# Layer 0's FFN sums through four PSUM banks, modulation products on ACT, layer 1's values and probabilities in float32

## The chip, the core and the metric

The kernel runs on one core of one Trainium2 chip. The core has TensorE (PE, with its own queue for weight loads, PEld), VectorE (DVE), ScalarE (ACT), GpSimd (POOL) and SyncE (SP), which here issues nearly all transfers from HBM, in the order of its queue. The metric is the time of one execution on the device in microseconds (us); less is better.

## The reference, cut to what matters

Two layers work on 512 latent tokens and 256 context tokens of width 1024. Both end in a SwiGLU FFN with 2816 hidden channels; layer 1's mixer is a differential attention with 8 heads of 2 x 64. In layer 1 the context gives only keys and values.

```
mx = silu(c) @ mod_w[l] + mod_b[l]          # shift, scale, gate, twice; the context has its own
h  = rms(x) * (1 + scale) + shift
q, k, v = split(h @ w_in)                   # layer 1, per head 2 x 64, 2 x 64 and 128
q, k = rope(rms(q) * qn), rope(rms(k) * kn) # rope on the latent tokens only
a  = softmax(q0 k0 / 8) - lam * softmax(q1 k1 / 8)
x  = x + gate1 * (rms(a @ v) * subln * (1 - lam_init)) @ w_out
x  = x + gate2 * ((silu(h @ w_gate) * (h @ w_up)) @ w_out)
```

## The kernel before, in words

The 768 tokens are six tiles of 128 (t = 4, 5 are the context). Nearly every product is made in three parts: weight and operand are each split into a high half (a cast to fp32r by ACT, L303 for weights, L397 for operands) and a low half (a subtraction by DVE or POOL, L304 and L398), and PE multiplies high by high, high by low and low by high. Attention weights times values in layer 0 are plain float32.

The order of the instructions on each engine is not written by hand: a scheduler with a cost model sets it from the order of the program, from priorities and from the number of buffers behind each tile name. SP issues transfers in the order it was given; one that waits for a buffer holds up all behind it.

The stages by time are layer 0's mixer (to about 450 us), layer 0's FFN (to 1048), layer 1's input projections and attention (1048 to 1400), its output projection and the norm before the FFN (to 1492) and layer 1's FFN (to the end).

The FFN (`ffn`, L710) goes over 22 blocks of 128 hidden channels in 11 passes of two. For each block PE makes the gate product `pg` and the up product `pu` (L738, 24 matmuls with 512 columns, and in layer 0 24 more with the context's 256) in two PSUM tiles of two banks each (`p_sc`, the names take turns). ACT makes Silu of `pg` into `sg`, DVE multiplies `sg` by `pu` (L753), and `split` makes the two halves `hdh` and `hdl`. Then each token tile and half of the columns gets its sum `dps` (L771 to L773, six matmuls of 512 columns, twelve in the last sums, which join two passes), in the banks `acc0` and `acc1` in turn. `residual` (L388) multiplies it by the gate into a tile `rtmp` in SBUF (DVE, L391) and adds that to x (L392: DVE, or POOL for the joined sums of layer 0). Two more PSUM banks, `tr0` and `tr1`, are there for transposes and small matmuls.

During layer 0's FFN the modulations of layer 1 are computed from 96 loads of 512 KB in all (`modw`, L191; some belong to the earlier path). `mod_chunks_by_pool` (L182) works for each chunk of 256 columns through two halves of the rows, for one or two streams (latent and context, the second in `modp`, one buffer; `modw` has two): POOL multiplies [128 x 4 x 256] by the conditioning vector (L197) and adds the four parts (L198 to L203) into `ma`. A matmul with ones (`modrow`, L208) sums over the partitions, ACT copies the row (L213), and a matmul turns it into columns (`modcol`, L216). `MODS1` gives the number of chunks for each pass: 2, 2, 2, 2, 2, 3, 3, 4, 4; the first eight chunks have two streams. There are 64 units of chunk, half and stream.

Layer 1 has a head's input projection (`in_proj1`, L571) for each token tile: the sum `inps` is copied to `qkv` by ACT, the values are split (`vv`: cast by ACT L594, subtraction by POOL L595), and `qk_norm_rope` squares (ACT, L358), reduces (DVE, L360), takes 1/sqrt on POOL (`rs_q`, L148 and L149), multiplies by it on DVE (L363), then multiplies by the rotation tables (`qz`, L372, and `qy`, L374, for queries and for keys each) and adds (L375). Queries and keys are then split and transposed on PE (`qpt`, L613, and `kpt`, L619). `attend1` (L625) makes two score tiles per head and latent tile, the exponentials `e` on ACT, their difference on DVE (L646), six transposes into `ppt`, a split of these into `PTh` and `PTl` (ACT and DVE), and the sum `av` (L653, L654) in six pairs of matmuls: `PTh` by both halves of the values side by side (256 columns) and `PTl` by the high half (128 columns). Two operations (ACT L656, DVE L658) join the two halves into `o`. Weights of the next head are loaded and split meanwhile (`wir`, L303 and L304).

## Time and profile before

| what | value |
|---|---|
| median of three runs | 1863.59 us (1863.56 to 1865.19) |
| profiled execution | 1865.25 us, its span 1863.5 us |
| PE busy | 1760.2 us (94%) |
| DVE, POOL, ACT busy | 1162.2, 789.8 and 716.5 us (62, 42 and 38%) |
| HBM read | 159.73 MB, 88 GB/s over the span |

The span is the time from the first to the last instruction in the trace; the rest of the profiled execution lies around it. Busy time counts an engine's own work, without its waits. The "chain that ended last" follows the work back from the last instruction. In the groups of instructions, the number behind the bar is the idle time of the engine just ahead of those instructions, with the instruction that ended it. "Granted clock" is the share of its full speed at which PE ran in a stretch.

### The profile page before, as it was taken

How to read it: one execution, taken by the hardware profiler on the slowest of the kernel's cores; microseconds unless marked ns; L12 is line 12 of the kernel's file. 1: busy time of each engine (PE TensorE's matmuls, PEld its weight loads, DVE VectorE, ACT ScalarE, POOL GpSimd, SP SyncE). 2: the span in 40 equal slices, each digit the busy share in tenths (PEclk: the TensorE clock that was granted, in tenths of full speed). 3: DMA queues.
4: the chain of work that ended last, by engine and by line, in shares of the span. 5: the costliest groups of instructions: out<-in, count | busy, mean ns of one | idle time of the engine just before them, and what ended most of it. 6: DMA issues, size and time to landing. Idle time of an engine off the chain costs nothing.

```text
span 1863.5 us, 25986 instructions
## 1 busy us (share of the span) xinstructions
PE 1760.2 (94%) x9910; PEld 1459.6 (78%) x9910; DVE 1162.2 (62%) x1927; ACT 716.5 (38%) x1470; POOL 789.8 (42%) x852
## 2 busy tenths in 40 slices
PE   6999999998999999899999889999998899999998
PEld 4877776666778888788888788999886688888887
DVE  4665455445268876667771767888876556566563
ACT  6556555434211112112211555676665332222220
POOL 2864545521099986735561655655543200000000
PEclk9999999999999999999999889999999899999999
DMA  9112222302533234424330211111103133223231
GB/s 314 42 41 77 83 93 91 100 23 81 180 114 101 93 100 146 138 91 136 103 124 14 96 38 57 35 38 48 49 19 107 46 113 108 85 91 113 69 113 46
DMA packets 152477, 165.64 MB, mean 89 GB/s; under 512 B 16480, under 2 KB 139936, under 8 KB 152352
## 3 DMA queue, kind: packets, MB, share of 16 engines
q1 hardware_dynamic: 152000, 163.77, 27.6%
q8 instruction: 78, 1.28, 0.3%
q14 instruction: 47, 0.39, 0.1%
q10 hardware_dynamic: 352, 0.21, 0.0%
HBM read 159.73 MB, written 4.22 MB: 88 GB/s over the span
## 4 chain that ended last, share of the span: by engine, by line
PE 74%; DVE 9%; ACT 5%; POOL 4%; DMA 3%; issue 3%; SPq 0%; POOLq 0%; ACTq 0%; DVEq 0%
PE pg L738 14%; PE pu L738 14%; PE dps L771 5%; PE dps L773 5%; PE dps L772 5%; PE inps L384 4%; PE inps L385 3%; PE inps L386 3%; PE av L548 3%; PE ppt L538 2%; PE sc L504 2%; PE ops L705 2%; PE ops L707 2%; PE ops L706 2%; PE av L653 1%
## 5 line engine op out<-in xcount | busy, mean ns | idle before, releaser
L738 PE MATMUL pg<-hT,wgh 128*128 128x512 f32 (+1 forms) x720 | 246.6, 391 | 3.1 <-ACT hT L288 3.1
L738 PE MATMUL pu<-hT,wuh 128*128 128x512 f32 (+1 forms) x720 | 243.2, 388 | 0.0
L391 DVE TENSOR_TENSOR rtmp<-dps,g 128x512 f32<-128x512 f32 x200 | 135.8, 687 | 163.7 <-PE dps L773 162.0
L392 DVE TENSOR_TENSOR x<-x,rtmp 128x512 f32<-128x512 f32 x188 | 198.8, 1065 | 3.8
L771 PE MATMUL dps<-wdh,hdh 128*128 128x512 f32 x440 | 177.1, 403 | 2.2 <-DVE rtmp L391 2.2
L772 PE MATMUL dps<-wdl,hdh 128*128 128x512 f32 x440 | 174.8, 397 | 0.0
L773 PE MATMUL dps<-wdh,hdl 128*128 128x512 f32 x440 | 171.9, 398 | 1.6 <-DVE hdl L398 1.6
L738 PEld LDWEIGHTS pg<-hT,wgh 128*128 128x128 f32 x720 | 135.4, 190 | 34.4 <-ACT hT L288 3.3
L738 PEld LDWEIGHTS pu<-hT,wuh 128*128 128x128 f32 x720 | 134.2, 188 | 29.6
L738 PE MATMUL pg<-hT,wgl 128*128 128x512 f32 (+1 forms) x360 | 141.4, 393 | 0.0
L738 PE MATMUL pu<-hT,wul 128*128 128x512 f32 (+1 forms) x360 | 139.7, 388 | 0.0
L384 PE MATMUL inps<-wih,hT 128*128 128x384 f32 x384 | 132.9, 346 | 0.4 <-ACT qkv L446 0.2
L397 ACT CAST hdh<-sg 128x768 fp32r<-128x768 f32 (+1 forms) x44 | 32.0, 728 | 256.5 <-DVE sg L753 256.5
L386 PE MATMUL inps<-wih,hT 128*128 128x384 f32 x384 | 130.3, 339 | 0.0
L385 PE MATMUL inps<-wil,hT 128*128 128x384 f32 x384 | 130.2, 339 | 0.0
L197 POOL TENSOR_TENSOR modw<-modw,cols 128x1024 f32<-128x1024 f32 x48 | 100.8, 2103 | 54.0 <-DMA modw<-in_mod_w_dram 53.7
L738 PE MATMUL pg<-hTc,wgh 128*128 128x256 f32 x352 | 99.5, 287 | 3.1 <-ACT hTc L288 2.4
L528 POOL TENSOR_SCALAR Pt<-Pt,rc 128x256 f32<-128x256 f32 (+3 forms) x96 | 69.2, 733 | 77.0 <-DVE rc L525 64.9
L771 PEld LDWEIGHTS dps<-wdh,hdh 128*128 128x128 f32 x440 | 83.2, 189 | 23.0 <-DVE rtmp L391 3.4
L773 PEld LDWEIGHTS dps<-wdh,hdl 128*128 128x128 f32 x440 | 83.0, 189 | 22.2 <-DVE hdl L398 2.3
L738 PE MATMUL pu<-hTc,wuh 128*128 128x256 f32 x352 | 98.1, 283 | 0.0
L772 PEld LDWEIGHTS dps<-wdl,hdh 128*128 128x128 f32 x440 | 83.3, 189 | 17.5
(230 smaller groups left out, 4486.3 us busy)
## 6 DMA issues: line engine op xcount, KB each, us to landing
modw<-in_mod_w_dram SPq DMA_DIRECT2D x96, 512.0 KB, 4.3
wgr<-in_ffn_w_in_dram SPq DMA_DIRECT2D x44, 512.0 KB, 3.4
wur<-in_ffn_w_in_dram SPq DMA_DIRECT2D x44, 512.0 KB, 3.5
wdr<-in_ffn_w_out_dram SPq DMA_DIRECT2D x44, 512.0 KB, 3.6
wir<-in_od_w_in_dram SPq DMA_DIRECT2D x96, 128.0 KB, 2.2
x<-in_x_dram SPq DMA_DIRECT2D x8, 512.0 KB, 3.5
wir<-in_ev_w_in_dram SPq DMA_DIRECT2D x16, 256.0 KB, 2.7
wor<-in_ev_w_out_dram SPq DMA_DIRECT2D x8, 512.0 KB, 4.3
```

Source lines behind the costliest of these rows:

```text
L197: nc.gpsimd.tensor_tensor(pr, w, bc(sk, 2, width), ALU.mult)
L384: nc.tensor.matmul(ps, hs[0][:, k, :], a, start=k == 0, stop=False)
L385: nc.tensor.matmul(ps, hs[0][:, k, :], b, start=False, stop=False)
L386: nc.tensor.matmul(ps, hs[1][:, k, :], a, start=False, stop=k == KT - 1)
L391: nc.vector.tensor_mul(tmp, ps, g[:, n * 512:(n + 1) * 512])
L392: eng.tensor_add(xt[:, n * 512:(n + 1) * 512], xt[:, n * 512:(n + 1) * 512], tmp)
L528: nc.gpsimd.tensor_scalar(p[:, :n], p[:, :n], rc[:, hh:hh + 1], 1.0, ALU.mult, ALU.mult)
L548: nc.tensor.matmul(av[64 * j:64 * j + 64, :], vv[:, vt[kc], :], PT[:, 2 * j:2 * j + 2].rearrange("p h q -> p (h q)"), start=kc == 0, stop= ...
L738: nc.tensor.matmul(ps[:, s0:s1], a, cols_T(b, s0, s1)[:, k, :], start=k == 0 and q == 0, stop=k == KT - 1 and q == 2)
L771: nc.tensor.matmul(ps, hh, a, start=j == 0, stop=False)
L772: nc.tensor.matmul(ps, hh, b, start=False, stop=False)
L773: nc.tensor.matmul(ps, hl, a, start=False, stop=j == nj - 1)
```

## The change

Four things are changed.

1. In both FFNs `sg` times `pu` is written back into `pu` in PSUM, and `split` reads it there; the residual multiplies `dps` in place and DVE adds it to x from PSUM (no `rtmp`, and no POOL adds for the joined sums). The sums of two blocks go through four banks, `acc0`, `tr0`, `acc1`, `tr1`; the joined sums keep two.
2. Of the modulations' work, the multiplications go from POOL (64 of 128 x 1024) to ACT (256 of 128 x 256, with a column of the conditioning vector as scale). The additions stay on POOL.
3. Layer 1's rotation tables hold all four 64-wide heads (two of queries, two of keys) with their norm weights (`head_tables`, in place of `rope_tables`), so that `rotate_all` has one multiplication for `qz` and one for `qy`, on the values that are not normalised yet. The multiplication by `rs_q` follows on POOL.
4. Layer 1's values are kept in float32 (a copy by POOL), and so are the transposed attention probabilities (the first four tiles copied by ACT, the last two by DVE). `av` is made of six float32 matmuls of 128 columns, and ACT alone scales it into `o`.

The scheduler orders the changed program anew. In layer 0's mixer PE's order stays as it was.

```diff
--- before.py
+++ after.py
@@ -75,7 +75,7 @@
     p_sc = es.enter_context(tc.tile_pool(name="p_sc", bufs=2, space=PSUM))
     dram = es.enter_context(tc.tile_pool(name="dram", bufs=1, space=bass.MemoryType.DRAM))
     p_1 = es.enter_context(tc.tile_pool(name="p_1", bufs=1, space=PSUM))
-    turn = {"acc": 0, "tr": 0}
+    turn = {"acc": 0, "tr": 0, "sum": 0}
 
     def phase_pool(name, side="left"):
         return tc.tile_pool(name=name, bufs=1, side=side, reuse_waits="tile")
@@ -193,8 +193,9 @@
                 for i, acc in reversed(list(enumerate(accs))):
 
                     pr = pool.tile([P, 4, width], F32, name="modp", tag="mp", bufs=1) if i else w
-                    sk = cols[:, 8 * i + 4 * pc:8 * i + 4 * pc + 4]
-                    nc.gpsimd.tensor_tensor(pr, w, bc(sk, 2, width), ALU.mult)
+                    for k in range(4):
+                        kk = 8 * i + 4 * pc + k
+                        nc.scalar.activation(pr[:, k], w[:, k], AF.Copy, scale=cols[:, kk:kk + 1])
                     nc.gpsimd.tensor_add(pr[:, 0:2], pr[:, 0:2], pr[:, 2:4])
                     if pc == 0:
                         nc.gpsimd.tensor_add(acc, pr[:, 0], pr[:, 1])
@@ -326,6 +327,45 @@
                                     rp[:, :, 1, :].rearrange("p t (a b) -> p t a b", b=2),
                                     bc(sw, 1, NTX), ALU.mult)
         return w, tb
+
+    def head_tables(pool, wq, wk, nq, nk):
+
+        rp = raw_tile([P, NTX, 2, HD], "rp")
+        nc.sync.dma_start(rp, rope)
+        n = nq + nk
+        w = pool.tile([P, 2, 2, HD], F32, name="rw", tag="rw")
+        nc.sync.dma_start(w[:, 0, 0, :], dram_rows(wq))
+        nc.sync.dma_start(w[:, 0, 1, :], dram_rows(wk))
+        nc.vector.tensor_scalar(w[:, 0, 0, :], w[:, 0, 0, :], HD ** -0.5, None, ALU.mult)
+        for j in range(2):
+            nc.vector.tensor_copy(w[:, 1, j, :].rearrange("p (a b) -> p a b", b=2), swap_pairs(w[:, 0, j, :]))
+        tb = pool.tile([P, NTX, 2, n, HD], F32, name="rt", tag="rt")
+        wc = pool.tile([P, n, HD], F32, name="rc", tag="rc")
+        for j, h0, m in ((0, 0, nq), (1, nq, nk)):
+            nc.vector.tensor_copy(wc[:, h0:h0 + m], bc(w[:, 0, j, :], 1, m))
+            for i in range(2):
+                wj = bc(bc(w[:, i, j, :], 1, m), 1, NTX)
+                nc.vector.tensor_tensor(tb[:, :, i, h0:h0 + m], bc(rp[:, :, i, :], 2, m), wj, ALU.mult)
+        return wc, tb
+
+    def rotate_all(raw, h0, n, t, wc, tb, pool):
+
+        sq = pool.tile([P, n * HD], F32, name="sq", tag="qz", bufs=2)
+        nc.scalar.activation(sq, raw, AF.Square)
+        ss = small.tile([P, n], F32, name="qss", tag="qss")
+        nc.vector.tensor_reduce(ss, sq.rearrange("p (h d) -> p h d", d=HD), AX.X, ALU.add)
+        r = rsqrt(ss, n, 1.0 / HD, "q")
+        y = pool.tile([P, n, HD], F32, name="qy", tag="qy", bufs=2)
+        rh = raw.rearrange("p (h d) -> p h d", d=HD)
+        if t >= NTX:
+            nc.vector.tensor_tensor(y, rh, wc[:, h0:h0 + n], ALU.mult)
+            return y, r
+        z = pool.tile([P, n, HD], F32, name="qz", tag="qz", bufs=2)
+        nc.vector.tensor_tensor(z.rearrange("p h (a b) -> p (h a) b", b=2),
+                                swap_pairs(raw), tb[:, t, 1].rearrange("p h (a b) -> p (h a) b", b=2), ALU.mult)
+        nc.vector.tensor_tensor(y, rh, tb[:, t, 0], ALU.mult)
+        nc.vector.tensor_add(y, y, z)
+        return y, r
 
     def rotate(raw, nq, nk, t, w, tb, pool):
 
@@ -351,30 +391,6 @@
         nc.vector.tensor_add(y, y, z)
         return y, r
 
-    def qk_norm_rope(ps, nq, nk, t, w, tb, pool):
-
-        n = nq + nk
-        sq = pool.tile([P, n * HD], F32, name="sq", tag="qz", bufs=2)
-        nc.scalar.activation(sq, ps[:, :n * HD], AF.Square)
-        ss = small.tile([P, n], F32, name="qss", tag="qss")
-        nc.vector.tensor_reduce(ss, sq.rearrange("p (h d) -> p h d", d=HD), AX.X, ALU.add)
-        r = rsqrt(ss, n, 1.0 / HD, "q")
-        y = pool.tile([P, n, HD], F32, name="qy", tag="qy", bufs=2)
-        nc.vector.tensor_tensor(y, ps[:, :n * HD].rearrange("p (h d) -> p h d", d=HD), bc(r, 2, HD), ALU.mult)
-        parts = [p for p in ((0, 0, nq), (1, nq, nk)) if p[2]]
-        if t >= NTX:
-            for j, h0, m in parts:
-                nc.vector.tensor_tensor(y[:, h0:h0 + m], y[:, h0:h0 + m], bc(w[:, j, :], 1, m), ALU.mult)
-            return y
-        z = pool.tile([P, n, HD], F32, name="qz", tag="qz", bufs=2)
-        for j, h0, m in parts:
-            sn = tb[:, j, t, 1, :].rearrange("p (a b) -> p a b", b=2)
-            nc.vector.tensor_tensor(z[:, h0:h0 + m].rearrange("p h (a b) -> p h a b", b=2),
-                                    swap_pairs(y[:, h0:h0 + m]), bc(sn, 1, m), ALU.mult)
-            nc.vector.tensor_tensor(y[:, h0:h0 + m], y[:, h0:h0 + m], bc(tb[:, j, t, 0, :], 1, m), ALU.mult)
-        nc.vector.tensor_add(y, y, z)
-        return y
-
     def project(ps, t, ws, c0, c1):
 
         hs = [tile_T(j, t) for j in range(2)]
@@ -397,22 +413,6 @@
         nc.scalar.copy(hi, src)
         nc.vector.tensor_sub(lo, src, f32(hi))
         return hi, lo
-
-    def transposed_probs(Pt, heads, tiles, pool):
-
-        res = []
-        per = 4 // heads
-        for g0 in range(0, len(tiles), per):
-            grp = tiles[g0:g0 + per]
-            m = len(grp)
-            pt = tr_tile("ppt", [P, per, heads, P])
-            for a, kc in enumerate(grp):
-                for hh in range(heads):
-                    nc.tensor.transpose(pt[:, a, hh, :], Pt[hh][:, kc * P:(kc + 1) * P], ident)
-            hi, lo = split(pool, pt[:, :m], [P, m, heads, P], "PT", 2)
-            for a in range(m):
-                res.append((hi[:, a], lo[:, a]))
-        return res
 
 
     def weights0(b, wp, sub, new_tile=raw_tile):
@@ -569,7 +569,7 @@
         return nlam
 
     def in_proj1(h, tabs, wp, st, wh, qp):
-        w, tb = tabs
+        wc, tb = tabs
         ws = []
         for u in range(4):
             def views(raw, u=u):
@@ -579,21 +579,22 @@
                         "(j p) n -> p j n", p=P)
             ws.append(unit(wh, views, [P, 2, 384], WBUF, "wi", nc.gpsimd if h or u % 2 else nc.vector))
         kT = st.tile([P, 2, TOK], F32R, name="kT", tag="kT")
-        vv = st.tile([P, NT, 2, P], F32R, name="vv", tag="vv")
+        vv = st.tile([P, NT, P], F32, name="vv", tag="vv")
         qs = {}
         late = None
         yield qs, kT, vv
         for t in CTX_FIRST:
-            nq = 2 if t < NTX else 0
-            n = 384 if nq else 256
+            h0 = 0 if t < NTX else 2
+            m = 4 - h0
+            n = 64 * m + P
             ps = acc_tile("inps", n, one=0) if h else p_sc.tile([P, 1024], F32, name="inps", tag="sc")[:, :n]
             project(ps, t, ws, 384 - n, 384)
             raw = wp.tile([P, 384], F32, name="qkv", tag="qkv", bufs=2)
             nc.scalar.copy(raw[:, :n], ps)
-            v = raw[:, n - P:n]
-            nc.scalar.copy(vv[:, t, 0, :], v)
-            nc.gpsimd.tensor_sub(vv[:, t, 1, :], v, f32(vv[:, t, 0, :]))
-            y = qk_norm_rope(raw, nq, 2, t, w, tb, wp)
+            nc.gpsimd.tensor_copy(vv[:, t, :], raw[:, n - P:n])
+            y, r = rotate_all(raw[:, :n - P], h0, m, t, wc, tb, wp)
+            nc.gpsimd.tensor_tensor(y, y, bc(r, 2, HD), ALU.mult)
+            nq = m - 2
             if nq:
                 qd = wp.tile([P, 2, 2, 2, HD], F32R, name="qd", tag="qd", bufs=2)
                 yb = bc(y[:, 0:2], 2, 2)
@@ -645,18 +646,24 @@
         nc.vector.scalar_tensor_tensor(rt, sm[:, 0:1], nlam, rc[:, 1:2], ALU.mult, ALU.mult)
         nc.vector.scalar_tensor_tensor(E[0], E[1], rt, E[0], ALU.mult, ALU.add)
         yield
-        PT = transposed_probs(E[:1], 1, list(range(NT)), mp)
-        av = acc_tile("av", 256, one=1)
+        av = acc_tile("av", P, one=1)
         vt = [4, 5, 0, 1, 2, 3]
-        for a, (hi, lo) in enumerate(PT):
-            v = vv[:, vt[a]].rearrange("p a d -> p (a d)")
-            nc.tensor.matmul(av, hi[:, 0], v, start=a == 0, stop=False)
-            nc.tensor.matmul(av[:, 0:P], lo[:, 0], v[:, 0:P], start=False, stop=a == len(PT) - 1)
+        for g0, m in ((0, 4), (4, 2)):
+            pt = tr_tile("ppt", [P, 4, P])
+            for a in range(m):
+                nc.tensor.transpose(pt[:, a, :], E[0][:, (g0 + a) * P:(g0 + a + 1) * P], ident)
+            PT = mp.tile([P, 4, P], F32, name="PT", tag="PT", bufs=3)
+            if g0:
+                nc.vector.tensor_copy(PT[:, :m], pt[:, :m])
+            else:
+                nc.scalar.copy(PT, pt)
+            for a in range(m):
+                kc = g0 + a
+                nc.tensor.matmul(av, PT[:, a, :], vv[:, vt[kc], :], start=kc == 0, stop=kc == NT - 1)
+        oc = o_t[t][:, h * P:(h + 1) * P]
+        nc.scalar.activation(oc, av, AF.Copy, scale=rc[:, 0:1])
+        ss = small.tile([P, 1], F32, name="oss", tag="oss")
         o1 = mp.tile([P, P], F32, name="o1", tag="o1", bufs=2)
-        nc.scalar.activation(o1, av[:, P:2 * P], AF.Copy, scale=rc[:, 0:1])
-        oc = o_t[t][:, h * P:(h + 1) * P]
-        nc.vector.scalar_tensor_tensor(oc, av[:, 0:P], rc[:, 0:1], o1, ALU.mult, ALU.add)
-        ss = small.tile([P, 1], F32, name="oss", tag="oss")
         nc.scalar.activation(o1, oc, AF.Square, accum_out=ss)
         r = rsqrt(ss, 1, 1.0 / P, "o")
         nc.vector.scalar_tensor_tensor(oc, oc, r, subln, ALU.mult, ALU.mult)
@@ -750,8 +757,9 @@
                 pg, pu = pg[:, :n_tok], pu[:, :n_tok]
                 sg = fp.tile([P, n_tok], F32, name="sg", tag="sg", bufs=1)
                 nc.scalar.activation(sg, pg, AF.Silu)
-                nc.vector.tensor_mul(sg, sg, pu)
-                hid.append(split(fp, sg, [P, n_tok], "hd", 4))
+
+                nc.vector.tensor_mul(pu, sg, pu)
+                hid.append(split(fp, pu, [P, n_tok], "hd", 4))
             for i, mod in enumerate(mods[0] if p == 0 and mods else ()):
                 mod_chunk(*mod, lambda shape, name: fp.tile(shape, F32, name=name, tag="mw", bufs=2), fp, f"tr{i % 2}", room=("ma", 4))
             if p and mods and mods[p]:
@@ -764,14 +772,18 @@
             nj = len(hid)
             for t in CTX_FIRST[:ntok] if ntok > NTX else range(ntok):
                 for n in range(2):
-                    ps = acc_tile("dps")
+                    if nj > 2:
+                        ps = acc_tile("dps")
+                    else:
+                        turn["sum"] = (turn["sum"] + 1) % 4
+                        ps = p_1.tile([P, 512], F32, name="dps", tag=("acc0", "tr0", "acc1", "tr1")[turn["sum"]])
                     for j in range(nj):
                         hh, hl = (z[:, t * P:(t + 1) * P] for z in hid[j])
                         a, b = (z[:, n * 512:(n + 1) * 512] for z in wo[j])
                         nc.tensor.matmul(ps, hh, a, start=j == 0, stop=False)
                         nc.tensor.matmul(ps, hh, b, start=False, stop=False)
                         nc.tensor.matmul(ps, hl, a, start=False, stop=j == nj - 1)
-                    residual(xs[t], ps, g[0 if t < NTX else 1], n, fp, nc.gpsimd if nj > 2 and l == 0 else nc.vector)
+                    residual(xs[t], ps, g[0 if t < NTX else 1], n)
                     if p == NF // 2 - 1:
                         done(t, n)
             wo, hid = [], []
@@ -932,7 +944,7 @@
     wp = Pool("mw1", "right")
     whi = Pool("whi", "right")
     wh = (whi.pool, wlo.pool)
-    tabs = rope_tables(wp.pool, od_qn[0], od_kn[0])
+    tabs = head_tables(wp.pool, od_qn[0], od_kn[0], 2, 2)
     fp.close()
     at = Pool("mix1")
     subln = at.pool.tile([P, P], F32, name="subln")
```

## The prediction

> **What bounds the kernel now.** I read the busy table and the chain of waits first, then one row per stage of the busy-time view (window in us, its length, then busy time of PE, PEld, DVE, ACT and POOL with counts, then the granted TensorE clock).
>
> ```profile
> PE 1760.2 (94%) x9910; PEld 1459.6 (78%) x9910; DVE 1162.2 (62%) x1927; ACT 716.5 (38%) x1470; POOL 789.8 (42%) x852
> ...
> PE 74%; DVE 9%; ACT 5%; POOL 4%; DMA 3%; issue 3%; SPq 0%; POOLq 0%; ACTq 0%; DVEq 0%
> ```
> ```profile
> 0.00:516.00 516.00, 474.36 (x3039) 357.03 (x3040) 256.58 (x583) 257.91 (x575) 221.21 (x302) 0.99 0.32 102
> 516.00:1048.00 532.00, 520.91 (x2746) 439.53 (x2745) 361.10 (x383) 103.00 (x120) 351.40 (x244) 0.99 0.33 104
> 1048.00:1160.00 112.00, 96.35 (x578) 90.65 (x577) 76.97 (x162) 60.67 (x148) 59.42 (x78) 0.86 0.22 65
> 1160.00:1384.00 224.00, 215.45 (x1493) 205.83 (x1492) 187.87 (x409) 151.43 (x418) 126.32 (x195) 1.00 0.12 36
> 1384.00:1492.00 108.00, 86.74 (x461) 70.88 (x461) 70.59 (x126) 53.26 (x105) 31.49 (x37) 0.91 0.22 75
> 1492.00:1863.50 371.50, 366.40 (x1604) 295.66 (x1602) 209.10 (x267) 90.23 (x106) 0.00 (x0) 1.00 0.29 92
> ```
>
> PE is the bound: layer 0's FFN (second row) has it busy 520.9 of 532 us, layer 1's FFN (last) 366.4 of 371.5. The change takes no matmul out of either. What can be won is PE's waiting: 11.1 us in the second row, 15.7 in the third (start of layer 1's attention), 8.6 in the fourth, 21.3 in the fifth, and the time in which the clock is low after a wait. Where those waits sit (same view), and the matmul that ended each (start, duration, [idle before <- releaser]):
>
> ```profile
> 552.00:560.00 8.00, 4.85 (x21) 3.23 (x20) 5.15 (x5) 0.37 (x1) 8.00 (x7) 0.88 0.13 38
> 760.00:784.00 24.00, 19.32 (x92) 15.88 (x91) 12.98 (x12) 5.79 (x7) 15.89 (x11) 0.86 0.51 169
> 1088.00:1140.00 52.00, 42.86 (x240) 40.34 (x240) 38.27 (x71) 27.86 (x70) 28.20 (x37) 0.80 0.18 51
> 1384.00:1426.00 42.00, 29.65 (x170) 23.71 (x170) 37.02 (x61) 28.84 (x66) 16.99 (x17) 0.88 0.34 115
> ```
> ```profile
> 557.85 0.92 PE L208 MATMUL modrow<-ma,cst 128*32 128x256 f32 x4 [3.15 <-POOL ma L203]
> ...
> 773.91 1.01 PE L216 MATMUL modcol<-cst,ma 64*128 64x2 f32 x4 [4.68 <-ACT ma L213]
> ...
> 1092.36 0.75 PE L613 MATMUL qpt<-identr,qd 128*128 128x128 f32 x4 [3.25 <-ACT qt L615]
> ...
> 1131.96 0.48 PE L654 MATMUL av<-vv,PTl 128*128 128x128 f32 x1 [2.93 <-DVE PTl L398]
> ```
>
> Idle plus (1 - clock) x length gives what each window loses: 3.15 + 0.96 = 4.1 at 552, 4.7 + 3.4 = 8.0 at 760, 9.1 + 10.4 = 19.5 at 1088, 12.35 + 5.0 = 17.4 at 1384. In the first POOL is busy all 8.00 us and PE waits for its accumulator; in the last DVE is busy 37.0 of 42.
>
> **The change, part by part.** The rows for costs (groups by line and shape: count | busy us, mean ns | idle before), the queue's own wait and the DMA issue:
>
> ```profile
> L392 DVE TENSOR_TENSOR x<-x,rtmp 128x512 f32<-128x512 f32 x188 | 198.8, 1065 | 3.8
> L391 DVE TENSOR_TENSOR rtmp<-dps,g 128x512 f32<-128x512 f32 x200 | 135.8, 687 | 163.7 <-PE dps L773 162.0 <-DMA g<-gmem 1.7
> L392 DVE TENSOR_TENSOR x<-x,ops 128x512 f32<-128x512 f32 x14 | 9.4, 680 | 0.3
> L398 DVE TENSOR_TENSOR hdl<-sg,hdh 128x768 fp32r<-128x768 f32 x22 | 30.8, 1400 | 3.7 <-ACT hdh L397 3.6
> L358 ACT ACTIVATE sq<-qkv 128x256 f32<-128x256 f32 x32 | 13.4, 418 | 0.0
> L197 POOL TENSOR_TENSOR modw<-modw,cols 128x1024 f32<-128x1024 f32 x48 | 100.8, 2103 | 54.0 <-DMA modw<-in_mod_w_dram 53.7
> L197 POOL TENSOR_TENSOR modp<-modw,cols 128x1024 f32<-128x1024 f32 x16 | 35.2, 2198 | 57.6 <-DMA modw<-in_mod_w_dram 57.6
> L304 POOL TENSOR_TENSOR wil<-wir,wih 128x768 fp32r<-128x768 f32 x42 | 79.5, 1898 | 18.7 <-ACT wih L303 17.4 <-PE kpt L619 0.8
> L449 POOL TENSOR_TENSOR qy<-qy,rs_q 128x320 f32<-128x320 f32 x24 | 17.3, 722 | 0.9
> ```
> ```profile
> SPq L191 <- POOL ma L200: 159.1, 18, 11.5
> ```
> ```profile
> modw<-in_mod_w_dram SPq DMA_DIRECT2D x96, 512.0 KB, 4.3
> ```
>
> 1. *Modulation products from POOL to ACT.* POOL loses 64 products, 100.8 + 35.2 = 136 of its 351.4 us in layer 0's FFN. ACT gets 4 x 64 = 256 activations of 128x256; the nearest row, 418 ns, makes 107 us on top of 103 in 532. Both engines then have slack in sum. The gain is that POOL no longer holds the weight buffers so long: SP's queue, in order, sat 159.1 us on POOL's first add, and behind it stand the FFN's weight loads, so that the cast of the down weights, and ACT's copy of the modulation row behind it, came late (the wait at 773.91). Per unit (half a chunk for one stream) POOL needs (351.4 - 136) / 64 = 3.4 us; the load takes 4.3 us, and two buffers through load, ACT (4 x .42 = 1.7) and adds (3.4) give (4.3 + 1.7 + 3.4) / 2 = 4.7 us. The products stand on ACT between the second hidden cast of one pass and the Silu of the next pass's first pair; queued behind them are that Silu, the casts of the next weights and the next hidden cast. PE needs that Silu when the gate and up products of the pair (2 x 24 x (.23 + .12) = 16.8) and the 72 sum matmuls of the pass before (16.6) are through, 33 us after its last up product; then the next gate product wants the bank. Ahead of the Silu stand 32 products (8 units, in the four passes with two streams) or about 20 (5 units, the later passes): 8 x 3.4 = 27 or 5 x 4.7 = 23.5 us, from about 3 us in (multiply, cast). So 27 to 30 of 33: hidden, with little room. The rows of PE's pitch:
>
> ```profile
> 839.74 0.39 PE L738 MATMUL pu<-hT,wuh 128*128 128x512 f32 x1
> 839.97 0.28 PE L738 MATMUL pu<-hTc,wuh 128*128 128x256 f32 x1
> 840.09 0.39 PE L738 MATMUL pu<-hT,wul 128*128 128x512 f32 x1
> ```
>
> From start to start 512 columns take .23 and 256 take .12 us. I take -11 for this part: both windows' 12.1 us less 1 for the small waits that take their place; bounds 0 (they refill) and -13 (all idle of the stage and the first windows' clock).
>
> 2. *Products and residuals in PSUM, four banks.* The add's row with the operand in SBUF is 1065 ns, with it in PSUM (x<-x,ops) 680: 188 x .385 = 72 us less on DVE, hidden beside PE (DVE 361 of 532 before); worth at most the 2 us of small waits that DVE ended there, taken as 0. A sum's bank is now held through multiply and add, but with four banks and 6 matmuls of .23 = 1.4 us a sum it has 4 us for 1.4. The last merged pass of layer 0 keeps two banks: 12 sums of 12 x .23 = 2.8 us, bank held .69 + .68 and, with what DVE has queued between multiply and add (up to four .4 us pieces), about 3.0; and the 12 adds come from POOL to DVE. That is .2 x 6 = +1 us; bounds 0 and 12 x .68 = +8. The product of gate and up stays in its bank until the split's low half (1400 ns here, from SBUF) has read it, some 2 us longer, of the 8.4 us that the next gate product gives before the next up product wants the bank: 0. Layer 1's FFN gets the same edit where PE waits for nothing of this: 0.
>
> 3. *Layer 1's queries and keys.* Tables are laid out for all four heads at once, so two pairs of 128-wide operations become two 256-wide ones; the normalisation is multiplied afterwards, by 32 (128x256) and 16 (128x128) new POOL operations; these at most .72 us each by the 320-wide row, 35 us, on POOL's 59 + 126 in 336, less 48 value splits that become copies of about the same length. DVE loses about 62 short pairs and the 25 + 25 low halves of the probabilities: by the rows of layer 1 some 70 us of 265. PE's waits at 1160 to 1384 (8.6 us) and 1384 to 1426 (12.35 + 5.0) are DVE's kind: DVE busy 188 of 224 and 37 of 42. I take 3 of 8.6 and 4 of 17.4: the end's work is one chain (norms, transposes, first weights) of which only the queue ahead shortens. Bounds 0 and everything, -26. At 1088 the wait is for the queries' transpose, behind r, y times r and, in POOL's new order, two weight splits of 1.9 us between them; so I take 1 of the 8 at 1092, and 3 of the 9 at 1132, whose low half of PT no longer exists. Bounds 0 and -19.5.
>
> 4. *Probabilities times values in float32.* Per head and tile six pairs of matmuls, 256 and 128 columns in fp32r, become six of 128 columns in float32; a float32 matmul leaves two records.
>
> ```profile
> 1207.09 0.34 PE L653 MATMUL av<-vv,PTh 128*128 128x256 f32 x1
> 1207.26 0.22 PE L654 MATMUL av<-vv,PTl 128*128 128x128 f32 x1
> 1207.32 0.33 PE L653 MATMUL av<-vv,PTh 128*128 128x256 f32 x1
> ```
> ```profile
> 302.61 0.65 PE L548 MATMUL av<-PT,vv 128*64 128x256 f32 x4
> 303.19 0.66 PE L538 MATMUL ppt<-cst,Pt 128*128 128x128 f32 x4
> ```
>
> A pair takes .23 us. Layer 0's float32 records go by at (303.19 - 302.61) / 4 = .145 with 256 columns; with 128 they lie between that and the fp32r pair's .23 / 2 = .115. Two records: .23 to .29, over 192 matmuls 0 to +11. I take +1, near the lower end: a loaded weight tile and half the columns. The Trainium skill's page "FP8 and Floating Point Precision", section "TensorE Precision Notes", gives true float32 four passes: 512 column passes against 384, an estimate of +.0575 x 192 = +11, the same upper end; the trace's two 256-column float32 matmuls in .58 us are 2.5 times, not four times, one fp32r pass of .12 each, so I give that little weight.
>
> Sum: -11 + 1 - 3 - 4 - 4 + 1 = -20. The profiled execution took 1865.25 us (span 1863.5 and 1.75 around it), 1.66 above the median of the runs, 1863.59; so 1845.25 for a profiled one and 1843.6 for the median.
>
> **The rivals.**
> *P, four passes.* As above, but the float32 matmuls cost the upper end: 1843.6 + 10 = 1854.
> *B, the waits of layer 1 go as well.* All of 19.5 at 1088 and most of the end's 17.4 and of the middle's 8.6: about -41 in all, 1822. For it: DVE loses a quarter of its work. Against: the transpose waits for r, which POOL computes.
> *C, ACT's queue becomes the wait.* At 4.2 us a unit the block ends at 3 + 8 x 4.2 = 36.6: 3.6 us late, with about 1 of clock (the loss at 552), in four passes, +18 and no -11: 1843.6 + 11 + 18 = 1873. At 4.0 us (2 late and 1, four times) it just eats the gain, 1855. For it: SP's wait shows how tightly this chain hangs on buffers. Against: ACT is busy 103 of 532, and the last unit's adds need not be waited for.
> *D, the other side: POOL in layer 1.* The multiply by r on POOL stands behind weight splits of 1.9 us that DVE's multiply was free of. If it makes each head's keys and queries late by 4 us (two splits), seven heads cost +28 and layer 1's gains of 11 go: 1843.6 + 28 + 11 = 1883. It decides from (20 - 11) / 7 = 1.3 us a head upwards. For it: PE waited 8 us at 1092 in just this place. Against: layer 0 has this order already (the 24 rows of 722 ns) and POOL is busy 126 of 224 us.
> *E, no change.* The waits return behind the loads: 1863.6.
>
> **How the numbers follow.** About 0.2% (3.7 us) is what a measurement can tell from no change. Chances: A (my sum) .51, P .05, B .10, C .14 (half of it slower, half still faster), D .12, E .08. Faster .51 + .05 + .10 + .07 = .73, same .08, slower .12 + .07 = .19. A's own range is 1832 to 1856: gains of parts 1 and 3 to their bounds, part 4 at its upper end. The range that holds 8 in 10 leaves out D and a little of B and C: 1819 to 1872.
>
> **What would show it right or wrong.** Right: in the window from 516 to 1048 POOL falls from 351 to about 215 us, ACT rises from 103 to about 210, PE's wait from 11 to about 2, and the stage ends some 11 us earlier; x<-x,dps rows on DVE at about 680 ns; the wait for modcol at 774 is gone. The float32 av rows follow each other at .11 to .12 us a record (P: .145). Wrong: PE rows released by ACT's sg or hdh in the passes with modulations (C); rows of qpt or kpt released by ACT or DVE behind POOL's y, more than 1.3 us a head (D); PE's idle at 1088 to 1140 under 3 us (B).

## The result and the profile after

The changed kernel takes 1841.17 us (median of four runs, 1836.81 to 1843.72) against 1863.57 us; the ratio is 0.9875, with a 95% interval of 0.9853 to 0.9897. The forecast was 1843.6 us. The profiled execution took 1842.98 us, with a span of 1841.2 us, 22.3 us below that of before.

The first lines of the profile of the changed kernel, busy time by engine:

```profile
PE 1755.7 (95%) x9910; PEld 1460.5 (79%) x9910; DVE 1026.1 (56%) x1767; ACT 802.6 (44%) x1646; POOL 621.8 (34%) x824
```

PE is still the bound, DVE has 136 us less and POOL 168. Where the 22.3 us lie is seen when both spans are cut at the same pieces of work: at layer 0's last up product, at layer 1's first projection and at the first gate product of layer 1's FFN. These are the matmuls at the cuts, and the last sum of each kernel; first the kernel before, then the changed one:

```profile
1011.58 0.28 PE L738 MATMUL pu<-hTc,wul 128*128 128x256 f32 x1
...
1049.53 0.48 PE L384 MATMUL inps<-wih,hTc 128*128 128x256 f32 x2
...
1481.03 0.58 PE L738 MATMUL pg<-hT,wgh 128*128 128x256 f32 x1 [3.08 <-ACT hT L288]
...
1858.55 0.40 PE L773 MATMUL dps<-wdh,hdl 128*128 128x512 f32 x1
```
```profile
995.01 0.28 PE L745 MATMUL pu<-hTc,wul 128*128 128x256 f32 x1
...
1035.46 0.50 PE L400 MATMUL inps<-wih,hTc 128*128 128x256 f32 x2 [0.21 <-ACT wih L304]
...
1455.36 0.58 PE L745 MATMUL pg<-hT,wgh 128*128 128x256 f32 x1 [2.90 <-ACT hT L289]
...
1836.28 0.40 PE L785 MATMUL dps<-wdh,hdl 128*128 128x512 f32 x1
```

The differences at the cuts are -16.6, -14.1, -25.7 and -22.3 us. By stage:

| stage | forecast | measured |
|---|---|---|
| layer 0's FFN, to its last up product | -11 | -16.6 |
| joined sums and norm, to layer 1's first projection | +1 | +2.5 |
| layer 1's attention and output projection | -4 -3 -4 +1 = -10 | -11.6 |
| layer 1's FFN | 0 | +3.4 |
| sum | -20 | -22.3 |

The busy time of the first and third stage, again before and then changed (columns as in the stage rows of the prediction):

```profile
516.00:1011.60 495.60, 485.06 (x2581) 410.52 (x2580) 340.49 (x343) 87.79 (x101) 331.88 (x223) 0.99 0.34 108
...
1049.50:1481.00 431.50, 389.95 (x2478) 359.29 (x2476) 326.66 (x681) 259.08 (x663) 213.69 (x305) 0.95 0.17 51
```
```profile
516.00:995.00 479.00, 479.00 (x2580) 407.88 (x2579) 250.08 (x343) 191.48 (x351) 164.34 (x160) 1.00 0.35 112
...
1035.40:1455.30 419.90, 385.08 (x2467) 357.31 (x2467) 275.74 (x501) 239.74 (x583) 231.31 (x352) 0.96 0.18 53
```

In layer 0's FFN PE now waits for nothing: 479.00 of 479 us busy at clock 1.00. POOL went from 332 to 164 us and ACT from 88 to 191. The new wait stands at the joined sums at the end of each FFN. The rows of the changed kernel that show it, PE's first and the groups behind them:

```profile
1002.63 0.50 PE L783 MATMUL dps<-wdh,hdh 128*128 128x512 f32 x1 [1.74 <-DVE x L408]
...
1819.61 0.50 PE L783 MATMUL dps<-wdh,hdh 128*128 128x512 f32 x1 [1.74 <-DVE x L408]
```
```profile
L407 DVE TENSOR_TENSOR dps<-dps,g 128x512 f32<-128x512 f32 x200 | 136.0, 697 | 137.5 <-PE dps L785 132.1 <-DMA g<-gmem 4.7
L408 DVE TENSOR_TENSOR x<-x,dps 128x512 f32<-128x512 f32 x200 | 133.4, 683 | 3.3
```
```profile
L198 ACT ACTIVATE modw<-modw,cols 128x256 f32<-128x256 f32 x192 | 82.3, 498 | 72.8 <-DMA modw<-in_mod_w_dram 64.2 <-POOL modw L199 4.2 <-POOL modw L203 2.2
L198 ACT ACTIVATE modp<-modw,cols 128x256 f32<-128x256 f32 x64 | 27.4, 499 | 27.6 <-POOL ma L204 15.1 <-DMA modw<-in_mod_w_dram 11.2 <-POOL ma L201 1.3
```

The releaser is the add out of the bank, as the two banks would have it. ACT's products took 82.3 + 27.4 = 110 us (one is 498 ns, but they overlap), against 107 forecast, and the adds 683 ns against 680.

### The profile page after: what moved, and what is told of

It reads as the page before. It is cut to its first block, busy times and chain, and to the rows that moved or that the text cites. A ratio compares the mean times of both kernels' runs of the same rounds, so it can differ in the third digit from the quotient of the medians.

```text
span 1841.2 us, 26076 instructions
## 1 busy us (share of the span) xinstructions
PE 1755.7 (95%) x9910; PEld 1460.5 (79%) x9910; DVE 1026.1 (56%) x1767; ACT 802.6 (44%) x1646; POOL 621.8 (34%) x824
## 5 line engine op out<-in xcount | busy, mean ns | idle before, releaser
L407 DVE TENSOR_TENSOR dps<-dps,g 128x512 f32<-128x512 f32 x200 | 136.0, 697 | 137.5 <-PE dps L785 132.1
L785 PE MATMUL dps<-wdh,hdl 128*128 128x512 f32 x440 | 166.9, 396 | 0.0
L408 DVE TENSOR_TENSOR x<-x,dps 128x512 f32<-128x512 f32 x200 | 133.4, 683 | 3.3
L198 ACT ACTIVATE modw<-modw,cols 128x256 f32<-128x256 f32 x192 | 82.3, 498 | 72.8 <-DMA modw<-in_mod_w_dram 64.2
L305 DVE TENSOR_TENSOR wul<-wur,wuh 128x1024 fp32r<-128x1024 f32 x44 | 53.9, 1225 | 80.6 <-ACT wuh L304 80.6
L761 DVE TENSOR_TENSOR pu<-sg,pu 128x768 f32<-128x768 f32 (+1 forms) x44 | 36.5, 829 | 109.4 <-PE pu L745 95.8
```

Source lines behind the costliest of these rows:

```text
L198: nc.scalar.activation(pr[:, k], w[:, k], AF.Copy, scale=cols[:, kk:kk + 1])
L305: (sub or nc.vector).tensor_sub(lo, raw, f32(hi))
L407: nc.vector.tensor_mul(tmp, ps, g[:, n * 512:(n + 1) * 512])
L408: eng.tensor_add(xt[:, n * 512:(n + 1) * 512], xt[:, n * 512:(n + 1) * 512], tmp)
L761: nc.vector.tensor_mul(pu, sg, pu)
L785: nc.tensor.matmul(ps, hl, a, start=False, stop=j == nj - 1)
```

## The experiments

Marks used below: the time of layer 0's last up product against the kernel before (-16.6 us in the changed one), and the time from head to head in the steady part of layer 1, from one head's first projection (`inps`, with the context's operand) to the next head's.

**One part undone each.** First, POOL multiplies the modulations again.

```diff
-                    for k in range(4):
-                        kk = 8 * i + 4 * pc + k
-                        nc.scalar.activation(pr[:, k], w[:, k], AF.Copy, scale=cols[:, kk:kk + 1])
+                    sk = cols[:, 8 * i + 4 * pc:8 * i + 4 * pc + 4]
+                    nc.gpsimd.tensor_tensor(pr, w, bc(sk, 2, width), ALU.mult)
```

> The changed kernel with one part undone: POOL multiplies the modulations again (64 multiplications of 128x1024), ACT has no products. Theory (the prediction's part 1): the 14 us by which layer 1's first projection started earlier (1035.5 against 1049.5 us) come from the products having left POOL and with them the weight loads behind SP's wait; undone, that projection starts at 1046 to 1050 and the time is 1852 to 1856 us. Rival: the 14 us come from the residuals in PSUM (DVE's add 683 instead of 1065 ns, and less on the memory that DVE and POOL share); then this kernel stays within 4 us of the changed one, 1837 to 1845, and PE's waits at 558 and 774 us do not come back.

Measured: 1846.48 us (1838.46 to 1849.74), ratio 0.9911. The profiled execution was the shortest, and there the last up product came 17.8 us earlier than in the kernel before, with POOL's multiplications back: the theory was wrong for this execution. The median was 5 us behind the changed kernel, between the two expectations. A second execution of the same kernel was profiled.

> The kernel with the products back on POOL once more, for a second profile: its times went from 1838 to 1850 us, and the profiled one was the shortest. Theory: in a longer execution one of layer 0's FFN waits is back (POOL 292 us busy of 495, near its due times), and the extra time stands ahead of layer 0's last up product. Rival: the extra time stands in layer 1 or is a lower clock throughout.

Measured: 1847.10 us, and the last up product 8.1 us earlier than before instead of 17.8: all of the extra time stands ahead of it, as the theory said. Against the first execution it is 9.7 us later. Of these, 2.8 were already there at 486 us; the other 6.9 came with one wait (PE, then DVE and POOL of the same execution):

```profile
598.66 0.76 PE L744 MATMUL pu<-hT,wuh 128*128 128x512 f32 x1 [4.24 <-DVE hdl L413]
```
```profile
580.16 13.43 DVE L304 TENSOR_TENSOR wgl<-wgr,wgh 128x1024 fp32r<-128x1024 f32 x1
593.51 0.67 DVE L407 TENSOR_TENSOR x<-x,dps 128x512 f32<-128x512 f32 x1
```
```profile
580.38 1.29 POOL L198 TENSOR_TENSOR modp<-modp 128x512 f32<-128x512 f32 x1
581.63 1.89 POOL L197 TENSOR_TENSOR modw<-modw,cols 128x1024 f32<-128x1024 f32 x1
...
590.61 1.89 POOL L197 TENSOR_TENSOR modw<-modw,cols 128x1024 f32<-128x1024 f32 x1
592.58 2.15 POOL L198 TENSOR_TENSOR modw<-modw 128x512 f32<-128x512 f32 x1
```

A weight split that takes about 1.2 us on DVE took 13.43 us, while POOL ran one instruction behind the other without a gap, at its full pace (its multiplications took 1.89 us here, 2.02 on average). DVE's product of gate and up, the low half `hdl` and PE stood behind it; from 598 to 604 us, with the wait just over, the granted clock was .50 to .51, which is the rest of the 6.9. So with the products on POOL the stage is at the edge: one of the two profiled executions has such a stretch, the other doesn't.

Second, the residuals, products and sums of the FFNs as before.

```diff
-                nc.vector.tensor_mul(pu, sg, pu)
-                hid.append(split(fp, pu, [P, n_tok], "hd", 4))
+                nc.vector.tensor_mul(sg, sg, pu)
+                hid.append(split(fp, sg, [P, n_tok], "hd", 4))
...
-                    if nj > 2:
-                        ps = acc_tile("dps")
-                    else:
-                        turn["sum"] = (turn["sum"] + 1) % 4
-                        ps = p_1.tile([P, 512], F32, name="dps", tag=("acc0", "tr0", "acc1", "tr1")[turn["sum"]])
+                    ps = acc_tile("dps")
...
-                    residual(xs[t], ps, g[0 if t < NTX else 1], n)
+                    residual(xs[t], ps, g[0 if t < NTX else 1], n, fp, nc.gpsimd if nj > 2 and l == 0 else nc.vector)
```

> The changed kernel with one part undone: products of gate and up, and residuals, go through SBUF again (rtmp), sums take two banks in turn, the joined sums of layer 0 are added by POOL. Theory: in the FFNs this part hides beside PE and costs at the joined sums at each end (2.5 to 5 us in layer 0, 2.2 in layer 1); undone, layer 0's last up product comes as early as in the changed kernel or up to 3 us later, the two ends are 4 to 7 us shorter, time 1834 to 1842 us. Rival: the relief of DVE and of the shared memory is what made layer 0's FFN faster: 1850 to 1856.

Measured: 1839.59 us (1837.94 to 1841.15), ratio 0.9877. The theory holds: the last up product is at -14.0 us, 2.6 behind the changed kernel, the time to layer 1's first projection is .3 us longer than before instead of 2.5, and layer 1's FFN .4 instead of 3.4.

**Both undone, and one alone.** Undoing either part left most of the gain. Two runs complete the square: the changed kernel with both parts undone (the two diffs above together), and the kernel before with the products on ACT alone (the first diff the other way round).

> The changed kernel with both FFN parts undone (products on POOL, rtmp and two banks); layer 1's change alone is left. Theory after the first experiments: each of the two parts by itself gives POOL enough room, so that undoing one showed little; with both undone PE's waits near 558 and 774 us return, layer 0's last up product is within 4 us of the kernel before, and the time is 1850 to 1855 us (1863 less layer 1's 11.6). Rival: layer 0's FFN gets faster by the new order alone that the scheduler finds for the changed program: 1837 to 1843.

> The kernel before with the products on ACT alone. Theory: layer 0's FFN loses its waits at 558 and 774 us by this part alone (last up product 13 to 17 us earlier), layer 1 keeps its own: 1847 to 1852 us. Rival: it needs the residuals in PSUM too: 1856 to 1863.

Measured: 1853.88 us (ratio 0.9937, 0.9921 to 0.9952) and 1852.08 us (0.9932, 0.9919 to 0.9946). Both theories hold, the second at the edge of its range. With both undone the last up product is at +.2 us and two waits are back, the first of them now for DVE's reading of a sum's bank and not for POOL; with products on ACT alone the wait at the column matmul is .76 us of 4.68, and the some 14 us won there (14.7 at the last up product) are still 14.0 at the last sum. PE's rows of the one and of the other:

```profile
551.17 0.50 PE L778 MATMUL dps<-wdh,hdh 128*128 128x512 f32 x1 [2.79 <-DVE rtmp L406]
...
773.70 0.50 PE L216 MATMUL modcol<-cst,ma 64*128 64x2 f32 x2 [3.72 <-ACT ma L213]
```
```profile
761.76 0.38 PE L217 MATMUL modcol<-cst,ma 64*128 64x2 f32 x2 [0.76 <-ACT ma L214]
```

| layer 0's last up product | products on POOL | products on ACT |
|---|---|---|
| residuals in SBUF | +.2 | -14.7, -14.0 |
| residuals in PSUM | -17.8, -8.1 | -16.6 |

Eight profiled kernels with both parts lie between -14.9 and -19.6 there, so differences of 2 or 3 us in the table say nothing. Either part can be enough to keep the stage's chains in time. One takes 136 us of work from POOL. The other takes away DVE's adds out of SBUF, and these and POOL's instructions lengthened each other: the adds took 1065 ns on average before and 807 with the products on ACT alone, POOL's multiplication 2103 ns before and 1990 in the first profile with the residuals in PSUM (next row). The second part also brings four banks for the sums and the product in PSUM, and no run takes these three apart. In the three profiles with the products on ACT no wait was over 2 us there.

```profile
L197 POOL TENSOR_TENSOR modw<-modw,cols 128x1024 f32<-128x1024 f32 x48 | 95.5, 1990 | 46.7 <-DMA modw<-in_mod_w_dram 46.7
```

**Layer 1's parts.** Both undone, and then the rotation alone undone (normalisation by DVE ahead of two tables, values and probabilities still float32; the diff is that of the second).

```diff
-    tabs = head_tables(wp.pool, od_qn[0], od_kn[0], 2, 2)
+    tabs = rope_tables(wp.pool, od_qn[0], od_kn[0])
...
-            y, r = rotate_all(raw[:, :n - P], h0, m, t, wc, tb, wp)
-            nc.gpsimd.tensor_tensor(y, y, bc(r, 2, HD), ALU.mult)
+            y = qk_norm_rope(raw, m - 2, 2, t, w, tb, wp)
```

> The changed kernel with layer 1's two parts undone (tables, order of the normalisation, values, probabilities, attention sums as before); the FFN parts stay. Theory: the changed kernel won 4.7 us at the start of layer 1's attention and 6.8 at its end, next to nothing between; undone these come back: 1851 to 1855 us. Rival: these gains only follow from what FFN 0 left (POOL free earlier, weights loaded earlier), and this kernel has them too: 1838 to 1845.

> The changed kernel with the rotation undone (the two tables of 64, normalisation by DVE ahead of it, pairs of 128-wide operations), values and probabilities in float32 kept. Theory: the gains of layer 1 come from the shorter path of the probabilities (no low half) and DVE's shorter queue, about half from each part: 1844 to 1849 us. Rival (the prediction's D in small): the multiplication on POOL behind the weight splits costs at the start of layer 1, where the changed kernel lost 3.4 us ahead of its second head; then this kernel is faster than the changed one, 1834 to 1840.

Measured: 1854.09 us (ratio 0.996, 0.9946 to 0.9974) with both undone, 1856.19 (0.9964, 0.9951 to 0.9977) with the rotation undone. Layer 1 gives its 11.6 us back in the first, as the theory said: its attention and output projection took 431.2 us there, 431.5 in the kernel before. The second fits neither expectation: with float32 alone the stage took 433.8 us, at 44.2 us a head, so by itself it is worth nothing. PE has no wait over .8 us in such a head (1205 to 1249 us), only several small ones and a granted clock of 0.96; what makes it slower stays open.

The other half was run too: rotation kept, values and probabilities split again (the small tile of the rotation's weights moved to a working buffer to make room).

```diff
-        w = pool.tile([P, 2, 2, HD], F32, name="rw", tag="rw")
+        w = raw_tile([P, 2, 2, HD], "rw")
...
-        vv = st.tile([P, NT, P], F32, name="vv", tag="vv")
+        vv = st.tile([P, NT, 2, P], F32R, name="vv", tag="vv")
...
-            PT = mp.tile([P, 4, P], F32, name="PT", tag="PT", bufs=3)
+        PT = transposed_probs(E[:1], 1, list(range(NT)), mp)
```

> The changed kernel with float32 undone in layer 1 (values and probabilities split again, sums in fp32r), the rotation kept; the rotation weights' small tile lies in a working buffer. Theory: the rotation carries the whole gain of layer 1, 1838 to 1845 us, and with the pairs' .24 instead of .22 us a little above the changed kernel. Rival: only both together shorten DVE's queue enough: 1849 to 1856.

Measured: 1857.63 us (ratio 0.9963, 0.995 to 0.9976), a little above the rival's range. It isn't a clean verdict: 13 us were lost already ahead of layer 1's first projection (PE waited 7.11 us for the norm), which the moved tile may have caused, and from that projection to the FFN it took 426.6 us, 4.9 less than before. But the heads took 42.5 us on average (39.0 to 44.2, from 1118.64 to 1330.99), against 41.2 before and 41.1 in the changed kernel. Neither half makes the steady part faster, and there DVE's work isn't what counts: DVE was busy 153.9 us from 1160 to 1340 us before, and 128.9 in the changed kernel, at the same pace.

**Where the normalisation is multiplied.**

```diff
-            nc.gpsimd.tensor_tensor(y, y, bc(r, 2, HD), ALU.mult)
+            nc.vector.tensor_tensor(y, y, bc(r, 2, HD), ALU.mult)
```

> The changed kernel, with layer 1's multiplication by the normalisation on DVE instead of POOL (32 of 128x256 and 16 of 128x128). Theory: on POOL it costs nothing in the steady part, and DVE's queue is what the rotation relieved: 20 us more on DVE make it 1842 to 1852 us. Rival (the prediction's D): behind POOL's weight splits it is late at the start of layer 1, and DVE is the better place: 1835 to 1840.

Measured: 1865.56 us (ratio 1.0004, 0.9994 to 1.0014): 24 us slower than the changed kernel, more than either expectation. DVE is busy for no larger share of the steady part: the rows from 1160 to 1340 us, of the changed kernel, of this one, and of the next experiment:

```profile
1160.00:1340.00 180.00, 172.46 (x1212) 165.43 (x1211) 128.87 (x228) 112.57 (x299) 113.66 (x186) 1.00 0.14 40
```
```profile
1160.00:1340.00 180.00, 165.63 (x1122) 160.05 (x1121) 129.02 (x237) 105.72 (x282) 95.68 (x147) 0.96 0.13 36
```
```profile
1160.00:1340.00 180.00, 177.32 (x1239) 172.09 (x1236) 121.05 (x265) 116.22 (x304) 74.30 (x144) 0.99 0.12 35
```

DVE is busy 128.9 and 129.0 of 180 us (29.4 and 31.8 us a head, as the heads are longer) and idle for over a quarter of the time in both, so it is not a full queue. PE idles 1.8 us more a head and is busy 1.4 us longer, at a granted clock of 0.96 instead of 1.00. What differs is seen in one head (all engines, of the kernel with the multiplication on DVE):

```profile
1214.47 1.80 POOL L305 TENSOR_TENSOR wil<-wir,wih 128x768 fp32r<-128x768 f32 x1
1214.53 2.02 DVE L596 TENSOR_TENSOR qy<-qy,rs_q 128x256 f32<-128x256 f32 x1 [1.18 <-POOL rs_q L149]
...
1217.04 0.36 PE L614 MATMUL qpt<-identr,qd 128*128 128x128 f32 x2 [2.87 <-ACT qd L601]
```

As soon as POOL has made `rs_q` it begins a weight split; DVE's multiplication by that same `rs_q` begins .06 us later and takes 2.02 us instead of .42, and PE waits 2.87 us for the queries. It comes back every 44.3 us, once a head (at 1172.72, 1217.04, 1261.36, 1305.67 and 1350.00). To tell this collision from a queue, the next run keeps the multiplication on DVE and leaves out POOL's splits from the second head on.

```diff
+        if sub == "none":
+            nc.scalar.copy(hi, raw)
+            return hi, hi
...
-            ws.append(unit(wh, views, [P, 2, 384], WBUF, "wi", nc.gpsimd if h or u % 2 else nc.vector))
+            ws.append(unit(wh, views, [P, 2, 384], WBUF, "wi", "none" if h else nc.gpsimd if u % 2 else nc.vector))
```

> The kernel with the normalisation's multiplication on DVE, and from layer 1's second head on the low halves of the weights left out (POOL subtracts nothing there; the matmuls with the low half read the high half in its place, so PE's work is the same and the values are not). Theory: on DVE the multiplication is late because POOL starts a weight split just then, and DVE's instruction of .42 us takes 2.02 while POOL runs, once a head; without the splits it takes .42 and PE's wait for the queries' transpose (2.6 to 3.0 us a head) goes: 41.1 us a head instead of 44.3, time 1838 to 1848 us. Rival: the wait comes from DVE's queue or from the 1/sqrt on POOL; then it stays 43.5 us or more a head, time 1858 to 1866.

Measured: 1828.72 us (ratio 0.9802, 0.9786 to 0.9817), below the range, because other waits went too: 40.2 us a head on average (39.3 to 42.5, from 1149.10 to 1310.11). All of DVE's multiplications took their .42 us in the steady part. The rows from 1160 to 1340 us, with the splits and without:

```profile
L596 DVE TENSOR_TENSOR qy<-qy,rs_q 128x256 f32<-128x256 f32 x17 | 13.6, 800 | 6.0 <-POOL rs_q L149 5.8
```
```profile
L599 DVE TENSOR_TENSOR qy<-qy,rs_q 128x256 f32<-128x256 f32 x18 | 7.6, 420 | 6.6 <-POOL rs_q L149 6.6
```

The theory holds, and the rival of a late 1/sqrt is out: DVE waited as long for `rs_q` in both (6.0 us over 17, 6.6 over 18). PE's order changed as well and POOL has less to do, so the whole 37 us between these two kernels aren't the price of that collision alone. Which of DVE's instructions POOL's split runs into is decided by the scheduler's order, and in the changed kernel these are others: from 1160 to 1340 us those over 1.3 us, but for one of 1.50, are the query's rotation ahead of its tables' sum, the context keys' product and the probabilities' difference, none of which PE waited for by more than .8 us.

**The joined sums.** The result's second and fourth stage point to the two banks. A version with `rtmp` for these sums alone:

```diff
-                    residual(xs[t], ps, g[0 if t < NTX else 1], n)
+                    residual(xs[t], ps, g[0 if t < NTX else 1], n, *((fp, nc.gpsimd if l == 0 else nc.vector) if nj > 2 else ()))
```

> The changed kernel, with rtmp in SBUF again for the joined sums alone (twelve matmuls, two banks), the adds of layer 0's joined sums on POOL. Theory: the waits for DVE's add at the end of both FFNs (1.74 us each, with the low clock behind them) go: PE's time from layer 1's FFN start to its last sum is 377.5 as before instead of 380.9, and the time is 1834 to 1839 us. Rival: the sums' end is not what costs there, 1840 to 1843.

Measured: 1838.03 us (1834.32 to 1839.32), ratio 0.9851 with an interval of 0.9835 to 0.9867. Both waits of 1.74 us fall to .55 (PE's rows):

```profile
1001.75 0.50 PE L783 MATMUL dps<-wdh,hdh 128*128 128x512 f32 x1 [0.55 <-DVE rtmp L407]
...
1815.43 0.50 PE L783 MATMUL dps<-wdh,hdh 128*128 128x512 f32 x1 [0.55 <-DVE rtmp L407]
```

Layer 0's end is hardly slower than before (+.3 against +2.5), and layer 1's FFN takes +1.5 us against +3.4, not all of it. This is the fastest complete kernel here. It is faster than the kernel before beyond doubt; its interval overlaps with that of the changed kernel, so against that one the trace speaks, not the times.

One more try on top of it, with the first head's weight splits all on DVE:

```diff
-            ws.append(unit(wh, views, [P, 2, 384], WBUF, "wi", nc.gpsimd if h or u % 2 else nc.vector))
+            ws.append(unit(wh, views, [P, 2, 384], WBUF, "wi", nc.gpsimd if h else nc.vector))
```

> The changed kernel with rtmp for the joined sums, and the first head's weight splits all on DVE. Theory: PE waited for POOL's split at the start of layer 1 (3.20 and 1.73 us in the changed kernel); on DVE the split takes .95 instead of 1.9 us and these waits halve: 1834 to 1837 us, against 1838.0 for the kernel with rtmp alone. Rival: DVE's queue is as late there: 1837 to 1842.

Measured: 1862.50 us (ratio 0.9987, 0.9978 to 0.9995), far outside both. The start of layer 1 is no worse, but then each head takes 44 to 46 us. The edit touches the first head only, but the scheduler's order changed for all of them, and now POOL's splits run into the low half of the queries, which PE needs next (DVE, POOL and PE of one head):

```profile
1204.49 4.37 POOL L305 TENSOR_TENSOR wil<-wir,wih 128x768 fp32r<-128x768 f32 x2 [0.18 <-ACT wih L304]
...
1207.12 2.02 DVE L602 TENSOR_TENSOR qd<-qy,qd 128x256 fp32r<-128x256 f32 x1
...
1209.19 0.49 PE L614 MATMUL qpt<-identr,qd 128*128 128x128 f32 x2 [2.84 <-DVE qd L602]
```

The first row holds two splits; the first takes 2.56 us, so the second begins at about 1207.05, just ahead of DVE's instruction.

## Why the prediction was right, and which of its steps were not

The direction, the time (1843.6 against 1841.17 us) and the two stages that gain were right. That the sum came so close is partly luck: terms that were off by -5.6 and -1.6 us met others that were off by +1.5 and +3.4. The steps:

1. *Products to ACT, -11.* The waits at 558 and 774 us went, ACT came out as reckoned, and POOL below it (332 - 136 = 196 us to the last up product, 164 measured: its adds became shorter as well, 1294 ns against 1624; they took 1389 with the products on ACT alone and 1451 with the residuals in PSUM alone):

```profile
L199 POOL TENSOR_TENSOR modw<-modw 128x512 f32<-128x512 f32 x48 | 62.1, 1294 | 68.7 <-ACT modw L198 64.0 <-PE dps L785 4.5
```

 The size was too small, past the step's own bound of -13: I counted the two windows' 12.1 us. The stage's own row has 10.5 us of idle time and a clock of 0.99, which over 495.6 us is another 5: together 15.5 of the 16.6. The loss outside the two windows was taken for one that would stay. And the cause was only half of it. The step put the residual's relief of DVE at 0; the square of four shows that it would have been enough by itself in some executions. Two sufficient causes, of which I saw one.
2. *Joined sums, +1 and 0.* The wait came where the step put it, in layer 0, and cost 2.5 us, inside its bounds (0 to 8). The step that failed is "Layer 1's FFN gets the same edit where PE waits for nothing of this: 0": its joined sums have the same two banks, and the row of before had the bank free after a multiplication of 687 ns. The run with `rtmp` there gave 1.9 of the 3.4 us back. The changed kernel's +3.4 is the highest of eight profiles with this FFN (+2.0 to +3.4); the two with `rtmp` for the joined sums have +1.5 and +1.8, the three with everything in SBUF -.1 to +.4. So the two banks have a part in it, and the products in PSUM or the four banks another; how large each is stays open.
3. *Layer 1, -11 in three waits.* The sum was right (-11.6 with the float32 part), its reasons were not. That DVE loses work did not carry the gain of the steady part: DVE was busy 154 of 180 us at 41.2 us a head before, and 129 of 180 both at 41.1 and at 44.3. What told those last two apart is which of DVE's instructions falls under a weight split of POOL; whether this also makes each half of the change alone slow was not shown. In the steady part I took 3 us of 8.6; it was .4 us over three heads (from the fifth head's first projection to the eighth's). The gain lay ahead of them and behind them, 4.7 and 6.5 us against 4 and 4. No run takes these two apart, so that they came out near the forecast does not show their reasons right.
4. *Float32 sums, +1.* Records of 128 columns went by at .11 us:

```profile
1194.87 0.68 PE L662 MATMUL av<-vv,PT 128*128 128x128 f32 x4
1195.31 0.31 PE L614 MATMUL qpt<-identr,qd 128*128 128x128 f32 x1
```

Four records in .44 us make .22 a matmul, against .23 for the pair before: about -2 us over 192, just below the lower bound, which I had set at the pair's own time. The rival's price of .29, layer 0's with 256 columns, did not come. Four passes aren't ruled out by that: the +.0575 reckoned for them was added to a pair that took .23 us for 384 columns, where the pitch of .23 for 512 gives .17. Four passes of 128 columns make .23 at that pitch, close to the .22; of layer 0's 256 columns they would make .46, and .29 was measured. How the time goes with the columns stays open.

Of the rivals, C (ACT's queue) did not show: PE waited for nothing from 516 to 995 us. B's 41 us came to 11.6. D, as written, was the wrong way round: POOL is the better place for the multiplication, because what collides with the weight split is an instruction of DVE, and POOL's own only queues behind it. The trace of before had the evidence (DVE's multiplication of 128x256 by `rs_q`, .42 us where nothing stood beside it, took 698 ns on average and 1.81 us at 1224.24), but the step read it as load. The edit that met the collision cost 24 us, more than any one part of this change won.

## What to carry to other kernels

A gain in a stage that an engine's queue feeds is read from the stage's whole row, idle time and clock together, not from its two largest waits. Where DVE and POOL both work out of SBUF, look at which of DVE's instructions stretch and who waits for those: the sum of busy time did not show it here, and where a scheduler sets the order, any edit can move the collision onto the critical chain, so each edit's trace is to be checked for it. When a result is moved from SBUF to PSUM, count how long its bank is now held at every place that uses it, the last and largest sums first.

## What the runs showed of the hardware

DVE's instructions with both operands in SBUF took 2.02 instead of .42 us beside one weight split on POOL, and once 13.43 instead of about 1.2 us beside a run of POOL instructions without a gap (12 us from 580.4 to 592.5), while POOL's multiplications kept their 1.89 us. With one operand in PSUM they kept their time (697 and 683 ns on average over 200 each). The Trainium skill's page "SBUF — State Buffer", section "Who interferes with whom", says that a DVE instruction with two inputs in SBUF contends with a GpSimd instruction that reads SBUF. The Trainium skill's same page, section "Summary: rules for kernel authors", says that the second of the two to issue blocks until the first is through. The first and the last of these numbers agree; in the 13.43 us the wait lasted over some ten of POOL's instructions, not one, which this rule alone doesn't say.
